# RWKV-7 time mixing: each direction's low-rank product issued by itself, between the preparation's own steps

## The chip, the core and the metric

The kernel runs on one core of one Trainium2 chip. The metric is the device time of one execution in microseconds (us): 2056.7 us is the median of three runs of the kernel before (2055.96 to 2057.23). Five engines of the core are spoken of: PE (TensorE, matmuls), ACT (ScalarE), DVE (VectorE), POOL (GpSimd) and SP (SyncE, which here issues most of the DMA transfers). Each engine works through its own queue in order.

## The reference, cut to what matters

Two trunk layers over 512 latent tokens and 256 context tokens. The first layer's mixer has an RWKV-7 half that runs in both directions `d` (forward, backward). Its preparation computes, per direction, a decay and an in-context learning rate, each through a low-rank product of inner width 64:

```
wl = wl.reshape(bn, s, 2, DECAY_LORA)        # DECAY_LORA = ICLR_LORA = 64
al = al.reshape(bn, s, 2, ICLR_LORA)
w_raw = prm['w0'] + jnp.einsum('bsdl,dlc->bsdc', jnp.tanh(wl), prm['w2'])
decay = jnp.exp(-jnp.exp(-jax.nn.softplus(-w_raw) - 0.5))
iclr = jax.nn.sigmoid(prm['a0'] + jnp.einsum('bsdl,dlc->bsdc', al, prm['a2']))
kk = (k * prm['k_k']).reshape(bn, s, A_HEADS, HEAD_DIM)
kk = kk / jnp.maximum(jnp.sqrt(jnp.sum(kk * kk, axis=-1, keepdims=True)), 1e-12)
```

The scan over the state then uses `w` (decay), `a` (iclr), `kk`, `k`, `r` and `v` of each direction. All the rest (the projections, windowed and other attention, two MLPs, the adaLN vectors from `w_ada`) is not touched.

## The kernel before

**Tiling.** Activations lie feature-major, 128 features on the partitions and T = 768 tokens (512 latent, 256 context) along the free axis. The eight RWKV heads are worked in four passes `p` of two heads (128 features). The two directions' low-rank inputs `wl` and `al` are 128x768 tiles: partitions 0 to 63 hold direction 0, partitions 64 to 127 direction 1. So the product of one direction reads one half of the partitions only.

**The preparation of a pass** is the generator `prep(p)` (L843): it loads `k` and `r` (L849, L850, on SP), forms the heads' inverse norms with `heads_rstd` (ACT square of `k`, L405 matmuls, L854 on DVE, a power on POOL, L412, L415 transposes) and `kk` (L856). Then come the lines of the change, L859 to L886: the low-rank products (L865), tanh and scaling on ACT, two scans on DVE (L877, L879) and the exponentials E and ei on ACT. After the mark FRONT it builds AR and BK (L903 to L908), products L917, the tile N by way of DRAM (L925, L928), and inverts 96 triangular 32x32 matrices in 31 steps of two DVE instructions (L954, L955). After the mark MERGE it joins the inverses (L974, L982 on PE).

**The recurrence of a pass** is `chunks(p)` (L989): four batches of three chunks, each `factors` (L1023 to L1040), `masked` (L1052, L1059), `own` (L1068), `solved` (L1077), and one batch later `local` (L1089, L1099, L1102), `passed` (L1012 to L1015 and, on DVE, L1116) and `step` (L1131 to L1138).

**What runs beside it.** The main loop walks `chunks(p)` and, at fixed rates, takes steps of `prep(p+2)`, of the output of pass p-1, and of `ada` (L332): the adaLN vectors, a product of 80 loads of `w_ada` in this stage, 512 KB each, that the rest of the stage does not need. Each load is one SP transfer (L341) into one of three buffers, is used by one group of four matmuls in the kernel's text (L353; 8 in the trace, where each such matmul stands twice), and every fourth group is followed by L362. I call one such group a filler below. The preparations of passes 0 and 1 run in the stage before, beside the input projection (L430); those of passes 2 and 3 beside `chunks(0)` and `chunks(1)`.

**What sets the order.** The kernel's text only gives a priority. A scheduler places every instruction into its engine's queue ahead of time, by what it expects to be ready; on the chip each queue then runs strictly in that order. In the recurrence stage PSUM has two tiles of two banks (`wide`), one bank for the fillers, and the recurrence's own.

Of the kernel before, what the change touches and what calls it, by code (L numbers as in the profile page):

```python
# [11 lines left out]
F32 = mybir.dt.float32  # L12
F32R = mybir.dt.float32r
AF = mybir.ActivationFunctionType
# [7 lines left out]
L = 512  # L22
CTX = 256
T = L + CTX
# [150 lines left out]
def trunk(ctx: ExitStack, tc: tile.TileContext, xT, cT, vec_d, wada, we, wo_in, wout, wf1, wf2, lw2_d, la2_d, lg2_d,  # L175
          rpb_d, con_d, nm_d, rot_d, out):
    nc = tc.nc
    V, S, G, PE = nc.vector, nc.scalar, nc.gpsimd, nc.tensor
    tt, ts, stt = V.tensor_tensor, V.tensor_scalar, V.scalar_tensor_tensor

    def act(o, i, f=AF.Copy, **k):
        return S.activation(o, i, f, **k)  # L182

    def pool(name, bufs=1, **k):
        return tc.tile_pool(name=name, bufs=bufs, reuse_waits="tile", **k)
# [26 lines left out]
    def one():  # L212
        if PS[0] is None:
            return wide()[:, 0:512]
        return PS[0].tile([128, 512], F32, name="x1")

    def wide():
        return PS[1].tile([128, 1024], F32, name="b2")
# [205 lines left out]
    def product(w, uh, ul, a, b, step=8):  # L424

        hi, lo = w
        ps = one()
        pairs = three(lambda k: hi[:, k, :], lambda k: lo[:, k, :], lambda k: uh[k][:, a:b], lambda k: ul[k][:, a:b], KT)
        for j, (x, y) in enumerate(pairs):
            PE.matmul(ps[:, 0:b - a], x, y, start=j == 0, stop=j == len(pairs) - 1)  # L430
            if j % step == step - 1 and j < len(pairs) - 1:
                yield
        return ps
# [409 lines left out]
    def prep(p, R, rt, iv, sts, res):  # L843

        def tmp():
            return rt.tile([128, T], F32, name="t", bufs=NT0)
# [9 lines left out]
        stt(kk, k, R["kkh"][:, p:p + 1], pb[0][:, :T], op0=ALU.mult, op1=ALU.mult)  # L856
        yield
        E, EI, IC = R["E"], [], []
        def lora(wt, src, bias, outs):  # L859

            ps = [wide() for d in range(2)]
            for a, b in ((0, L), (L, T)):
                for d in range(2):
                    ds = slice(d * 64, d * 64 + 64)
                    PE.matmul(ps[d][:, a:b], wt[ds, p * 128:(p + 1) * 128], src[ds, a:b], start=True, stop=True)  # L865
            for d in range(2):
                act(outs[d], ps[d][:, :T], AF.Tanh, scale=0.5, bias=R["w0h"][:, bias + d * 4 + p:bias + d * 4 + p + 1])
            return outs
        lds = lora(R["lw2"], R["wl"], 0, [tmp() for d in range(2)])
        yield  # L870
        for d in range(2):
            ld = lds[d]
            act(ld, ld, AF.Identity, scale=-0.5 * EM05, bias=R["ldc"])
            yield
            cum = rt.tile([128, T], F32, name=f"ei{d}")
            if d == 0:
                V.tensor_tensor_scan(cum, R["scan"], ld, 0.0, op0=ALU.mult, op1=ALU.add)  # L877
            else:
                V.tensor_tensor_scan(cum[:, ::-1], R["scan"], ld[:, ::-1], 0.0, op0=ALU.mult, op1=ALU.add)  # L879
            yield  # L880
            if not d:
                IC += lora(R["la2"], R["al"], 8, [rt.tile([128, T], F32, name=f"ic{e}") for e in range(2)])
                yield
            act(E[d][:, :, 1:65], c3(cum), AF.Exp)
            act(cum, cum, AF.Exp, scale=-1.0)
            EI.append(cum)  # L886
            yield
# [33 lines left out]
        for d in range(2):  # L921
            for b in range(2):
                o = d * 64 + b * 32
# [26 lines left out]
        for s in range(31):  # L950
            a, b = s + 1, 31 - s
# [10 lines left out]
        for d in range(2):  # L962
            for b in range(2):
                o = d * 64 + b * 32
# [312 lines left out]
    def front(p):  # L1277

        if p < 4:
            preps[p] = prep(p, R, rt, iv, sts, res)  # L1280
            yield from until(preps[p], FRONT)
# [6 lines left out]
    with psum(2, 2), pool("pat", 2, space=PSUM) as pat, pool("wp", side="right") as wp, pool("ub", 1, side="right") as ub:  # L1288
# [127 lines left out]
        R = mix_setup(mixs[1].enter_context(pool("rc")))  # L1416
        btx = ExitStack()
        with pool("po", 1, side="right") as pp:
# [17 lines left out]
            for n, m in enumerate(ms[:3]):  # L1436
                ps = one()
# [9 lines left out]
            while next(cg, "end") != "end":  # L1447
                n += 1
                due += RATE1 if ab else RATE2
                while due >= 1:  # L1450
                    due -= 1
                    if ab and next(ab, "end") == "end":
                        ab = None
                        btx.close()
                        rt, iv = (mixs[q].enter_context(pool(("rt", "iv")[q - 2])) for q in (2, 3))
# [6 lines left out]
            if ab:  # L1462
                drain(ab)
                btx.close()
                rt, iv = (mixs[q].enter_context(pool(("rt", "iv")[q - 2])) for q in (2, 3))
# [281 lines left out]
    with ExitStack() as p3:  # L1747
# [13 lines left out]
        with pool("po", 1) as pp:  # L1761
            ws = [W.take() for _ in range(4)]
            po = [pp.tile([128, T], F32, name=f"po{m}") for m in range(6)]
            for ms, gs in ((range(4), GROUPS[:2]), ((4, 5), GROUPS[:2]), ((0, 1), GROUPS[2:])):
                for c, tok in gs:
                    while c == 1 and pend:
                        tick()
                    for m in ms:
                        if m == len(ws):
                            ws.append(W.take())  # L1770
                        p = product(ws[m], *u1, tok.start, tok.stop, 12)
# [119 lines left out]
```

## Time and profile before

| what | value |
|---|---|
| three runs, median (lowest, highest) | 2056.7 us (2055.96, 2057.23) |
| the profiled execution, its own time | 2055.19 us |
| span of that execution | 2053.4 us |
| mean granted clock of TensorE | 0.971 |
| PE busy | 1932.7 us, 94% of the span |
| DVE / ACT / POOL busy | 1124.7 / 817.0 / 122.2 us |
| recurrence of pass 0 / 1 / 2 / 3 begins (first L974) | 357.0 / 448.3 / 549.9 / 622.3 us |
| the output stage's first matmul (L1588) | 691.3 us |

The profile page gives busy times over the whole span; since stages differ, the rows quoted further down are taken by stretches of time, given in us from the start of the span. "[0.96 <-DVE t L412]" behind a row means that the engine sat idle for 0.96 us just before it, and that the wait ended with that instruction. A matmul row with xN merges N instructions. Names in the rows are the program's tile names without their buffer numbers. The L numbers are lines of the kernel before.

### The profile page before, as it was taken

How to read it: one execution, taken by the hardware profiler on the slowest of the kernel's cores; microseconds unless marked ns; L12 is line 12 of the kernel's file. 1: busy time of each engine (PE TensorE's matmuls, PEld its weight loads, DVE VectorE, ACT ScalarE, POOL GpSimd, SP SyncE). 2: the span in 40 equal slices, each digit the busy share in tenths (PEclk: the TensorE clock that was granted, in tenths of full speed). 3: DMA queues.
4: the chain of work that ended last, by engine and by line, in shares of the span. 5: the costliest groups of instructions: out<-in, count | busy, mean ns of one | idle time of the engine just before them, and what ended most of it. 6: DMA issues, size and time to landing. Idle time of an engine off the chain costs nothing.

```text
span 2053.4 us, 38620 instructions
## 1 busy us (share of the span) xinstructions
PE 1932.7 (94%) x16412; PEld 1633.5 (80%) x16412; DVE 1124.7 (55%) x1999; ACT 817.0 (40%) x1531; POOL 122.2 (6%) x149
## 2 busy tenths in 40 slices
PE   6999988988888899999999999899999899999997
PEld 3878767666666897888888889898888798888887
DVE  6576477547464377233433345856575575444445
ACT  3466442534335244311322122435686645222332
POOL 1000011011100000000000000001021000000000
PEclk9999989999999999999999999999999999999998
DMA  7422334666634233211221021342111334322221
GB/s 309 149 65 78 108 109 129 209 195 207 207 126 145 71 112 132 73 61 42 83 72 62 32 83 42 103 151 68 51 39 37 123 102 166 102 83 82 97 88 42
DMA packets 112013, 217.47 MB, mean 106 GB/s; under 512 B 38496, under 2 KB 63968, under 8 KB 111328
## 3 DMA queue, kind: packets, MB, share of 16 engines
q1 hardware_dynamic: 96544, 191.66, 28.6%
q10 hardware_dynamic: 15296, 23.33, 3.2%
q8 instruction: 129, 2.11, 0.4%
q14 instruction: 44, 0.36, 0.1%
HBM read 184.29 MB, written 28.05 MB: 103 GB/s over the span
## 4 chain that ended last, share of the span: by engine, by line
PE 63%; DVE 7%; ACT 3%; issue 3%; DMA 2%; POOL 1%; POOLq 0%; ACTq 0%; DVEq 0%; SPq 0%
PE x L1588 45%; PE x L430 5%; PE ax L530 2%; PE ax L511 2%; PE b L1015 1%; PE b L493 1%; PE ad L353 1%; PE b L1077 1%; PE b L494 1%; DMA w_raw<-in_wada_dram 1%; DVE X L955 1%; DVE nacc L288 1%; ACT Z L182 1%; DVE pr L954 1%; POOL r L264 0%
## 5 line engine op out<-in xcount | busy, mean ns | idle before, releaser
L182 ACT ACTIVATE w_hi<-w_raw 128x1024 fp32r<-128x1024 f32 x183 | 192.3, 1058 | 484.1 <-PE x L1588 369.1
L225 DVE TENSOR_TENSOR w_lo<-w_raw,w_hi 128x1024 fp32r<-128x1024 f32 x181 | 220.8, 1223 | 194.6 <-ACT w_hi L182 193.0
L1588 PE MATMUL x<-fl,w_hi 128*128 128x256 f32 (+1 forms) x864 | 290.9, 338 | 3.9 <-DVE fl L1675 3.9
L1588 PE MATMUL x<-uh,w_hi 128*128 128x512 f32 (+1 forms) x864 | 286.7, 337 | 3.0 <-ACT uh L182 3.0
L1588 PE MATMUL x<-fh,w_lo 128*128 128x256 f32 (+1 forms) x864 | 289.4, 336 | 0.0
L1588 PE MATMUL x<-ul,w_hi 128*128 128x512 f32 (+1 forms) x864 | 287.9, 336 | 0.0
L1588 PE MATMUL x<-uh,w_lo 128*128 128x512 f32 (+1 forms) x864 | 287.6, 336 | 0.0
L1588 PE MATMUL x<-fh,w_hi 128*128 128x256 f32 (+1 forms) x864 | 286.9, 337 | 0.0
L1602 DVE TENSOR_TENSOR oa<-x,oa 128x512 f32<-128x512 f32 (+1 forms) x184 | 103.1, 563 | 207.9 <-PE x L1588 207.0
L430 PE MATMUL x<-uh,w_hi 128*128 128x256 f32 (+1 forms) x560 | 190.2, 340 | 1.6 <-ACT po L182 1.3
L430 PE MATMUL x<-uh,w_lo 128*128 128x256 f32 (+1 forms) x560 | 189.1, 338 | 0.0
L430 PE MATMUL x<-ul,w_hi 128*128 128x256 f32 (+1 forms) x560 | 188.5, 337 | 0.0
L1588 PEld LDWEIGHTS x<-fl,w_hi 128*128 128x128 f32 x864 | 164.3, 190 | 22.0 <-DVE fl L1675 4.3
L1588 PEld LDWEIGHTS x<-uh,w_hi 128*128 128x128 f32 x864 | 161.8, 189 | 21.1 <-ACT uh L182 3.9
L1588 PEld LDWEIGHTS x<-fh,w_lo 128*128 128x128 f32 x864 | 164.1, 190 | 17.9
L1588 PEld LDWEIGHTS x<-fh,w_hi 128*128 128x128 f32 x864 | 162.1, 190 | 20.0 <-ACT fh L182 2.5
L1588 PEld LDWEIGHTS x<-ul,w_hi 128*128 128x128 f32 x864 | 162.8, 189 | 17.7
L1588 PEld LDWEIGHTS x<-uh,w_lo 128*128 128x128 f32 x864 | 162.8, 189 | 17.6
L430 PEld LDWEIGHTS x<-uh,w_hi 128*128 128x128 f32 x560 | 107.5, 192 | 12.5 <-issue 2.7
L430 PEld LDWEIGHTS x<-uh,w_lo 128*128 128x128 f32 x560 | 107.7, 192 | 9.4 <-issue 1.2
L430 PEld LDWEIGHTS x<-ul,w_hi 128*128 128x128 f32 x560 | 107.8, 192 | 9.2 <-issue 1.3
L1674 DVE TENSOR_TENSOR rl<-rl 128x512 f32<-128x512 f32 (+1 forms) x108 | 59.3, 550 | 77.7 <-ACT fh L182 77.5
(304 smaller groups left out, 3398.7 us busy)
## 6 DMA issues: line engine op xcount, KB each, us to landing
w_raw<-in_wf_dram SPq DMA_DIRECT2D x128, 512.0 KB
w_raw<-in_wada_dram SPq DMA_DIRECT2D x96, 512.0 KB
w_raw<-in_we_dram SPq DMA_DIRECT2D x21, 512.0 KB
w_raw<-in_wo_in_dram SPq DMA_DIRECT2D x18, 512.0 KB
w_raw<-in_wout_dram SPq DMA_DIRECT2D x16, 512.0 KB
hsc<-h ACTq DMA_DIRECT2D x8, 1024.0 KB
scr<-po ACTq DMA_DIRECT2D x21, 384.0 KB
h<-hsc SPq DMA_DIRECT2D x7, 1024.0 KB
```

The costliest lines, as they stand in the source:

```text
L182: return S.activation(o, i, f, **k)
L225: eng.tensor_tensor(o_lo, x, o_hi.bitcast(F32), op=ALU.subtract)
L288: V.tensor_reduce(acc, sq.rearrange("p k t -> p t k"), axis=AX.X, op=ALU.add)
L353: PE.matmul(ps[o:o + 32, 0:256], si[:, 2 * kp + k, :], w[:, k, j * 256:(j + 1) * 256], start=kp == 0, stop=kp == 3)
L430: PE.matmul(ps[:, 0:b - a], x, y, start=j == 0, stop=j == len(pairs) - 1)
L493: PE.matmul(ps[:, off:off + n], qs, kh, start=True, stop=False)
L494: PE.matmul(ps[:, off:off + n], qs, kl, start=False, stop=True)
L511: PE.transpose(pt[:, (kb - k0) * 128:(kb - k0 + 1) * 128], P[:, kb * 128:(kb + 1) * 128], ident)
L530: PE.matmul(po[h * 64:h * 64 + 64, 0:128], v(h, k), pts[h][:, k], start=k == 0, stop=k == n - 1)
L1588: PE.matmul(o, a, b, start=n == 0, stop=n == len(pairs) - 1)
L1602: tt(oa[:, m, tok], ps, oa[:, m, tok], op=ALU.add)
L1674: tt(r, r, r, op=ALU.mult)
```

## The change

`lora` computed one kind of product for both directions: four matmuls, the two directions in turn for the 512 and then the 256 columns, into two `wide` tiles, followed by both tanh. It now computes one direction: two matmuls into one `wide` tile and one tanh. The decay product of direction 1 is issued after the whole chain of direction 0 instead of before it, and each direction's learning-rate product follows its own scan. The number of matmuls, activations, scans and steps (`yield`) is the same.

```
-        def lora(wt, src, bias, outs):
-            ps = [wide() for d in range(2)]
-            for a, b in ((0, L), (L, T)):
-                for d in range(2):
-                    ds = slice(d * 64, d * 64 + 64)
-                    PE.matmul(ps[d][:, a:b], wt[ds, p * 128:(p + 1) * 128], src[ds, a:b], start=True, stop=True)
-            for d in range(2):
-                act(outs[d], ps[d][:, :T], AF.Tanh, scale=0.5, bias=R["w0h"][:, bias + d * 4 + p:bias + d * 4 + p + 1])
-            return outs
-        lds = lora(R["lw2"], R["wl"], 0, [tmp() for d in range(2)])
-        yield
         for d in range(2):
-            ld = lds[d]
+            ds = slice(d * 64, d * 64 + 64)
+            def lora(wt, src, bias, o):
+                ps = wide()
+                for a, b in ((0, L), (L, T)):
+                    PE.matmul(ps[:, a:b], wt[ds, p * 128:(p + 1) * 128], src[ds, a:b], start=True, stop=True)
+                act(o, ps[:, :T], AF.Tanh, scale=0.5, bias=bias)
+                return o
+            ld = lora(R["lw2"], R["wl"], R["w0h"][:, d * 4 + p:d * 4 + p + 1], tmp())
             act(ld, ld, AF.Identity, scale=-0.5 * EM05, bias=R["ldc"])
             yield
...
-            if not d:
-                IC += lora(R["la2"], R["al"], 8, [rt.tile([128, T], F32, name=f"ic{e}") for e in range(2)])
-                yield
+            IC.append(lora(R["la2"], R["al"], R["w0h"][:, 8 + d * 4 + p:8 + d * 4 + p + 1], rt.tile([128, T], F32, name=f"ic{d}")))
+            yield
             act(E[d][:, :, 1:65], c3(cum), AF.Exp)
```

The scheduler places the rest of the stage anew. Lines behind the change carry numbers that are lower by five now (L1077 is L1072, L1099 is L1094, L1102 is L1097).

**Place 1, SP, from the load of `v` of pass 0 on.** `k`, `r` and `v` are loads of the recurrence and of the preparation of pass 2, `lg` and `gl` of the gate, `nscr` and `N` the way of pass 1's tile through DRAM, `w_raw<-in_wada` the loads of the fillers. Before:

```order
L1000 DMA v<-scr 128x768
L849 DMA k<-scr 128x768
L836 DMA lg_3421<-in_lg_dram 128x512
L838 DMA gl<-scr 128x768
L341 DMA w_raw<-in_wada_dram 128x1024 x2
L925 DMA nscr<-XI 32x24x32 x4
L341 DMA w_raw<-in_wada_dram 128x1024 x2
L928 DMA N<-nscr 96x1024
L341 DMA w_raw<-in_wada_dram 128x1024 x7
L850 DMA r<-scr 128x768
```

The same place on SP now:

```order
L995 DMA v<-scr 128x768
L836 DMA lg_3421<-in_lg_dram 128x512
L838 DMA gl<-scr 128x768
L341 DMA w_raw<-in_wada_dram 128x1024
L920 DMA nscr<-XI 32x24x32 x4
L341 DMA w_raw<-in_wada_dram 128x1024 x2
L923 DMA N<-nscr 96x1024
L341 DMA w_raw<-in_wada_dram 128x1024 x8
L849 DMA k<-scr 128x768
L850 DMA r<-scr 128x768
```

The load of `k` of pass 2, second in this row before, now stands behind eleven more filler loads; counted from the program's start, seven filler loads stand ahead of it before, and eighteen now.

**Place 2, PE, in `chunks(0)`, from the end of the first batch (`solved`) on.** L405 is the product of `heads_rstd` of pass 2, which reads the square of that `k`. Before:

```order
L1077 MATMUL b_3868<-XA,XI 64x128 x12
L405 MATMUL b_3886<-con,t 128x2 x6
L1023 MATMUL b_3903<-con,bk_2657 128x128 x3
L1023 MATMUL b_3903<-con,bk_2658 128x128 x3
L1099 MATMUL py<-Z,BT 64x64
L1029 MATMUL b_3913<-con,ar 128x128 x3
L1040 MATMUL b_3913<-con,vr 128x128 x3
L1099 MATMUL py<-Z,BT 64x64
L415 MATMUL b_3930<-con,t 128x128
```

The same place on PE now:

```order
L1072 MATMUL b_3868<-XA,XI 64x128 x12
L1094 MATMUL py<-Z,BT 64x64 x2
L353 MATMUL ad<-w_raw,si 32x256 x4
L1094 MATMUL py<-Z,BT 64x64 x2
L1097 MATMUL py<-Z,BT 64x64 x8
L353 MATMUL ad<-w_raw,si 32x256 x12
L362 MATMUL ad<-con,adar 128x4 x2
L353 MATMUL ad<-w_raw,si 32x256 x16
L362 MATMUL ad<-con,adar 128x4 x2
L353 MATMUL ad<-w_raw,si 32x256 x8
L405 MATMUL b_3886<-con,t 128x2 x6
L1018 MATMUL b_3903<-con,bk_2657 128x128 x3
```

Ten fillers (40 matmuls of the text) in one row now stand between `solved` and L405, where none stood; fillers 9 to 18 of the stage. Nine fillers precede L405 before, eighteen now. At the next such place, L405 of pass 3, the count is 46 in both.

**Place 3, PE, in the second batch of `chunks(0)`: the low-rank products of pass 2.** Two `wide` tiles at once before (b_4091 is direction 0, b_4092 direction 1):

```order
L1068 MATMUL b_4069<-Z,AK 64x64 x5
L865 MATMUL b_4091<-al,la_469 128x512
L865 MATMUL b_4092<-al,la_469 128x512
L865 MATMUL b_4091<-al,la_469 128x256
L353 MATMUL ad<-w_raw,si 32x256 x4
L865 MATMUL b_4092<-al,la_469 128x256
```

The same place on PE now (b_4061 is `al` of direction 0, b_4106 `wl` of direction 1):

```order
L1010 MATMUL b_4039<-BT,XA 64x128 x8
L865 MATMUL b_4061<-al,la_469 128x512
L865 MATMUL b_4061<-al,la_469 128x256
L1063 MATMUL b_4069<-Z,AK 64x64 x12
L362 MATMUL ad<-con,adar 128x4 x2
L1126 MATMUL pd<-Nb,MQ 64x64
L865 MATMUL b_4106<-wl,lw_468 128x512
L353 MATMUL ad<-w_raw,si 32x256 x4
L865 MATMUL b_4106<-wl,lw_468 128x256
L1072 MATMUL b_4111<-XA,XI 64x128 x12
```

In passes 2 and 3 all four products now stand apart, with other work between them. In passes 0 and 1 the scheduler puts `al` of direction 0 and `wl` of direction 1 next to each other, so two of the four products still have a neighbour on the other half of the partitions.

## Rows read from the trace of the kernel before

**Rows 1.** The page: the PE line of its first part, the GB/s line of its second (40 equal slices of the span), and the shares by engine of the chain that ended last.

```profile
PE 1932.7 (94%) x16412; PEld 1633.5 (80%) x16412; DVE 1124.7 (55%) x1999; ACT 817.0 (40%) x1531; POOL 122.2 (6%) x149
...
GB/s 309 149 65 78 108 109 129 209 195 207 207 126 145 71 112 132 73 61 42 83 72 62 32 83 42 103 151 68 51 39 37 123 102 166 102 83 82 97 88 42
...
PE 63%; DVE 7%; ACT 3%; issue 3%; DMA 2%; POOL 1%; POOLq 0%; ACTq 0%; DVEq 0%; SPq 0%
```

**Rows 2.** Busy time by stretches of the recurrence stage: the stretch, its length, busy us (instructions) of PE, PEld, DVE, ACT, POOL, then the granted clock, the DMA share and GB/s.

```profile
357.00:374.00 17.00, 14.71 (x349) 12.09 (x345) 4.80 (x10) 8.09 (x16) 0.46 (x2) 0.70 0.66 182
...
392.00:420.00 28.00, 25.80 (x446) 17.52 (x444) 22.81 (x61) 13.14 (x24) 0.37 (x1) 1.00 0.82 275
...
374.00:478.00 104.00, 91.60 (x1704) 62.91 (x1702) 60.31 (x141) 43.30 (x83) 12.86 (x13) 0.97 0.69 213
...
625.00:691.00 66.00, 56.08 (x1218) 45.93 (x1218) 31.92 (x42) 34.84 (x60) 4.87 (x5) 0.92 0.32 108
```

**Rows 3.** The low-rank products alone (L865) by stretches: PE busy us (instructions), PEld, granted clock, DMA share, GB/s. First one product of one direction of pass 0 by itself, then all four of pass 1, then the two pairs of pass 2 and the two pairs of pass 3.

```profile
253.00:255.50 2.50, 1.55 (x4) 0.67 (x4) 0.99 0.00 0
287.00:300.00 13.00, 9.83 (x16) 4.47 (x16) 0.51 0.03 12
382.00:386.00 4.00, 1.89 (x8) 0.66 (x8) 1.00 0.65 198
396.00:400.00 4.00, 2.47 (x8) 1.07 (x8) 1.00 0.76 253
491.00:494.00 3.00, 2.21 (x8) 1.15 (x8) 1.00 0.54 175
500.00:504.00 4.00, 2.68 (x8) 0.97 (x8) 1.00 0.67 241
```

**Rows 4.** PE in order of time: start, us, instruction, count, and in brackets the idle time before it and what ended it. Two low-rank products of pass 0; the end of the first batch of `chunks(0)` and the start of the second; a wait later in `chunks(0)`; and the same places of `chunks(1)`.

```profile
249.38 1.22 PE L865 MATMUL b<-wl,lw 64*128 64x512 f32 x1
...
249.39 1.22 PE L865 MATMUL b<-al,la 64*128 64x512 f32 x1
...
372.53 1.53 PE L1077 MATMUL b<-XA,XI 64*64 64x128 f32 x24 [0.59 <-ACT XA L182]
373.99 1.17 PE L405 MATMUL b<-con,t 128*128 128x2 f32 x9
...
376.55 0.33 PE L1099 MATMUL py<-Z,BT 128*64 128x64 f32 x2
...
378.91 0.30 PE L415 MATMUL b<-con,t 128*128 128x128 f32 x1 [0.96 <-DVE t L412]
...
382.21 0.63 PE L1102 MATMUL py<-Z,BT 128*64 128x64 f32 x15
...
432.17 0.38 PE L1131 MATMUL pd<-x,MQ 64*64 64x64 f32 x5 [2.23 <-DVE MQ L1116]
...
467.52 1.53 PE L1077 MATMUL b<-XA,XI 64*64 64x128 f32 x24
...
470.07 0.33 PE L1099 MATMUL py<-Z,BT 128*64 128x64 f32 x2 [0.21 <-ACT Z L182]
...
478.23 2.67 PE L405 MATMUL b<-con,t 128*128 128x2 f32 x12 [1.26 <-ACT t L182]
```

**Rows 5.** SP in order of time (start, us over which the merged issues lie, what is issued): `k` of pass 2, filler loads, and the store of pass 1's inverses.

```profile
350.23 0.34 SPq L849 DMA_DIRECT2D k<-scr  x1
...
354.27 2.06 SPq L341 DMA_DIRECT2D w_raw<-in_wada_dram  x2
...
364.14 25.55 SPq L341 DMA_DIRECT2D w_raw<-in_wada_dram  x7
...
414.49 0.34 SPq L959 DMA_DIRECT2D xscr<-X  x1
```

**Rows 6.** The chain that ended last, in order of time: start, us, what; transfers that work waited for from issue to landing.

```profile
441.54 5.57 DMA w_raw<-in_wada_dram
...
473.30 3.92 DMA k<-scr
...
542.33 4.47 DMA w_raw<-in_wada_dram
...
583.99 5.76 DMA w_raw<-in_wada_dram
```

**Rows 7.** What PE waited for from 374 to 478 us: us in total, times, longest.

```profile
PE ad L353 <- DMA w_raw<-in_wada_dram: 3.4, 4, 1.3
PE pd L1131 <- DVE MQ L1116: 2.6, 2, 2.2
```

**Rows 8.** The last reader of pass 1's `k` on POOL, the square of pass 2's `k` on ACT, and the first step of pass 1's inverse on DVE, in order of time.

```profile
348.40 1.80 POOL L940 TENSOR_TENSOR t<-ic,k 128x768 f32<-128x768 f32 x1 [8.69 <-DVE bk L908]
...
353.38 0.94 ACT L182 ACTIVATE t<-k,vec 128x768 f32<-128x768 f32 x1 [3.91 <-DVE ar L945]
...
381.44 0.18 DVE L954 TENSOR_TENSOR pr<-X,N 96x31 f32<-96x31 f32 x1
```

**Rows 9.** The fillers alone from 374 to 478 us: the matmuls L353, and in the second row L362; the columns of Rows 3.

```profile
374.00:478.00 104.00, 24.32 (x296) 6.02 (x296) 0.97 0.69 213
...
374.00:478.00 104.00, 5.37 (x36) 4.70 (x36) 0.97 0.69 213
```

## The prediction

> **What bounds the kernel now.** I read the page first, then stretches, then PE in order of time. PE is busy 94% of the span and holds 63% of the chain that ended last [rows 1]; the shares don't tell what a change inside one stage is worth, so the stretches come next. From 374 to 478 us, where the preparation of pass 2 runs beside `chunks(0)`, PE is busy 91.6 of 104 us; in the last pass, with no filler left, 56.1 of 66 [rows 2]. The stage therefore ends with PE's work plus PE's gaps, and those gaps are short: 3.4 us on filler loads and 2.6 on the tile MQ in these 104 us [rows 7]. The other engines have room, DVE 60 of 104 us [rows 2]. Whatever lengthens PE's work here, or stops its queue, delays every later stage one for one, since PE goes on to the output stage in the same queue.
>
> **Part 1: the products lose their neighbour.** One direction's product alone takes 1.55 us at the full clock (2.4 GHz), so four apart take 6.2. Side by side, the two pairs of pass 2 take 1.89 + 2.47 = 4.36 us and those of pass 3 2.21 + 2.68 = 4.89 [rows 3]. Apart, the passes gain 1.84 and 1.31 us of PE work, 3.15 in all. Passes 0 and 1 gain nothing: in pass 0 `wl` of direction 1 and `al` of direction 0, two separate calls, already ran at the same time (249.38 and 249.39) [rows 4], and they stay neighbours; in pass 1 all four take 9.83 us at half clock [rows 3], two pairs' worth of overlap before and one before the other in the new order alike. The bounds of this part are 0 (it falls into gaps) and 3.15; I take 3.15, since PE has few gaps at these places.
>
> The rows say that a pair costs 1.89 to 2.68 us where one product costs 1.55, so the overlap is partial. The Trainium skill ("TensorE: Matmul & The Clock Gate", Measured speedup vs the span model) would let row-packed matmuls finish in the time of one plus some 4 ns for each further tile. By that page a pair would take 1.55 us and the split would cost 3.1 us a pass, an estimate of 6.2 in all instead of 3.15; no pair here shows it, and the measurement decides.
>
> What the split may win: one `wide` tile at a time instead of both, an earlier tanh, shorter holds of the `t` buffers. The trace has no gap of note that these would end, so 0. In pass 0 DVE gets two L945 ahead of L903 and L908 of direction 1, up to 1 us of wait for L917; with direction 0's BK earlier in exchange I take 0, between -1 and +1.
>
> **Part 2: the load of `k` moves, and PE's queue stops for it.** Before, `k` of pass 2 was issued at 350.23, right after its buffer's last reader on POOL, and its square was ready at 354.3 [rows 5, 8], 20 us before PE came to L405 at 373.99 [rows 4]. Now SP issues it behind eleven more filler loads. A filler load waits until a buffer is given back by the filler three places earlier, so SP cannot reach `k` until PE has done filler 15. On PE fillers 9 to 18 stand in a row ahead of L405, and behind L405 everything waits: L1023 and all of the second batch on PE; on ACT the square of `k` stands ahead of that batch's BT; on DVE the norm stands amid pass 1's inverse.
>
> Walk it through. Only three filler buffers exist, so fillers 9, 10 and 11 have their data and 12 to 18 must be loaded within the row. PE reaches the end of `solved` some 1.0 us earlier, since one filler at half clock moved behind it: L1077 starts at 371.5. L1099 starts 2.55 us after the start of L1077, as in `chunks(1)` (467.52, 470.07) [rows 4]: 374.05; filler 9 is done and its buffer free by 375.0. A load takes 4.47 to 5.76 us from issue to landing where work waited for it [rows 6]; take 4.5: 379.5. The next six follow at the pace of the DMA: 0.524 MB at 275 GB/s, the rate of the busiest stretch [rows 2], is 1.9 us each: 390.9. `k` (0.393 MB) takes 1.4 us more: 392.3; its square 0.94 [rows 8]: L405 starts at 393.2, 19.2 us later than before. By then PE has done ahead of time nine fillers at 24.32 / 37 = 0.66 us, two groups L362 at 5.37 / 9 = 0.60 [rows 9], and L1099 and L1102, some 1.2 us [rows 4]: 8.3 us. The stall is 19.2 - 8.3 = 10.9 us net.
>
> Bounds: with 3.92 us to the first landing [rows 6], 309 GB/s [rows 1], so 1.7 us each, and `k` landing with the last load, L405 starts at 390.0 and 7.7 us are lost. With 5.76, 2.1 us each (three buffers, (5.76 + 0.66) / 3) and 3.92 for `k` after the last load, it starts at 398 and 15.9 are lost. I take 10.9, nearest to the busiest measured stretch.
>
> Here the rate is what a page would price otherwise. The rows show 275 GB/s in the busiest stretch. The Trainium skill ("DMA: Bandwidth & Descriptors", Anatomy of one DMA) fits a transfer as 2.0 us plus its bytes at 436 GB/s. By that, an estimate, a load lands 3.2 us after its issue and the next ones 1.2 apart, L405 starts at 387.2 and the stall is 4.9 us; the loads of 4.5 to 5.8 us in this trace speak against it.
>
> **What is given back, and the clock.** The same number of fillers lies between here and L405 of pass 3, so 9 fewer come later. Of PE's 12.4 us of gaps in these 104 us some end: a filler now stands by the 2.23 us wait for MQ [rows 4], two of the waits around L362 move into the row, and pass 1's inverse, which started at 381.44 behind `kk` of pass 2 [rows 8] and was stored at 414.49 [rows 5], is done before the second batch and leaves DVE free. But `chunks(1)` starts with fewer fillers to cover its own waits. Between 0 and 9 us; I take 4. The clock: after a wait of 1.26 us and others before it L405 of pass 3 took 2.67 us [rows 4], and the stretch from 357 to 374 had a granted clock of 0.70, a mix of 2.4 and 1.2 GHz [rows 2]. Behind 10 us of idling the first work will run at 1.2 GHz: 0 to 5 us, I take 1.2, the excess of that one L405.
>
> **The sum.** 3.15 + 10.9 + 1.2 - 4 = 11.3 us. The profiled execution took 2055.2 us, so 2066.5; the median of the runs stands 1.5 above it: 2068. The ends: 0 + 7.7 + 0 - 9 gives no loss, which I count with the rivals; 3.15 + 7.7 + 0 - 9 = 1.9, so 2058.6; 3.15 + 15.9 + 5 - 0 = 24, so 2081.
>
> **The rivals.** (a) The burst runs faster than its neighbours in the trace: nothing else is under way on the DMA, loads follow at 1.7 us, `k` lands with the last. 7.7 + 3.15 - 3.2 = +7.6: 2064. For it: the transfers of 309 GB/s at the start; against it: 4.5 us and more to landing wherever work waited. The page's fit above points this way. (b) The stall is moved, not added: the gaps behind it close, since fillers are then far ahead and DVE is free. 10.9 + 3.15 - 9 = +5, and with the faster burst +2: 2059 to 2062. Against it: most gaps are waits within the recurrence that no filler covers. (c) The other side: the early inverse and the burst buy back more than they cost. It decides where the gaps ended exceed the stall plus the products' excess: with a stall of 7.7, the products hidden, and all 12.4 us of gaps gone, 4.7 us faster: 2052. Against it: `chunks(1)` followed `chunks(0)` without waiting for the inverse, so an earlier one brings nothing by itself. (d) Worse: `k` lands late behind `r` and the loads, and the clock stays at 1.2 GHz for ten microseconds more: +18 to +24: 2075 to 2081. (e) The queue's new order does nothing, since loads run far enough ahead: 2057. Three buffers speak against it.
>
> **How the numbers follow.** A measurement of this kernel can tell some 0.2%, 4.1 us, from no change. Forecast 0.48, (a) 0.15, (b) 0.16, (c) 0.07, (d) 0.10, (e) 0.04. Slower by over 0.2%: 0.48 + 0.15 + 0.10 and half of (b), 0.81; within: half of (b) and (e), 0.12; faster: 0.07. The range takes in the forecast's bounds, (a), (b) and most of (d): 2058 to 2079.
>
> **What would show it.** Right: L405 of pass 2 near 393 us, behind fillers that wait for `w_raw`, the row from L1077 to L405 with some 10 us of idle PE; products of 1.55 us each in passes 2 and 3; `chunks(1)` and all later stages 10 to 12 us later. Wrong: L405 before 385, or the start of the output stage near 691 in spite of a late L405 (gaps closed), or fillers that start without a wait.

## The result, and the profile after

| | kernel before | changed kernel |
|---|---|---|
| median of 6 runs each (lowest, highest) | 2055.93 us (2052.72, 2057.23) | 2075.64 us (2068.53, 2080.87) |
| ratio, 95% interval | | 1.0103, 1.0086 to 1.0119 |
| profiled execution, its own time; span; clock | 2055.19; 2053.4; 0.971 | 2068.53; 2066.4; 0.964 |
| `chunks(0)` begins (first L974, now L969) | 357.1 us | 360.1 us |
| L405 of pass 2 | 374.0 | 394.3 |
| `chunks(1)` begins | 448.3 | 464.1 |
| `chunks(2)` begins | 549.9 | 564.1 |
| `chunks(3)` begins | 622.3 | 635.1 |
| output stage begins (L1588, now L1583) | 691.35 | 706.49 |

Slower, by 19.7 us in the medians, within the range. The execution that left the profile was the shortest of its six: 13.3 us longer than the profiled one of before. The table says where these 13.3 us arise: 3.0 are there when the recurrence begins, 12.7 come in `chunks(0)`, the rest stays within 2.5 us a stage in both signs. Not all of the 12.7 is lost time: six fillers and one L362, some 4.6 us at the rates of [rows 9], are done in `chunks(0)` now and later before (five of the six in `chunks(1)`, one in `chunks(2)`).

The place that the prediction walked through, PE in order of time, answering to [rows 4]:

```profile
373.02 1.53 PE L1072 MATMUL b<-XA,XI 64*64 64x128 f32 x24 [0.59 <-ACT XA L182]
375.56 0.33 PE L1094 MATMUL py<-Z,BT 128*64 128x64 f32 x2 [1.02 <-ACT Z L182]
...
377.63 1.07 PE L353 MATMUL ad<-w_raw,si 128*32 128x256 f32 x16
380.19 0.64 PE L353 MATMUL ad<-w_raw,si 128*32 128x256 f32 x8 [1.49 <-DMA w_raw<-in_wada_dram]
381.34 0.61 PE L362 MATMUL ad<-con,adar 128*128 128x4 f32 x4 [0.50 <-ACT adar L182]
382.91 2.30 PE L353 MATMUL ad<-w_raw,si 128*32 128x256 f32 x16 [0.97 <-DVE X L950]
385.59 1.08 PE L353 MATMUL ad<-w_raw,si 128*32 128x256 f32 x8 [0.38 <-DMA w_raw<-in_wada_dram]
388.08 1.08 PE L353 MATMUL ad<-w_raw,si 128*32 128x256 f32 x8 [1.41 <-DMA w_raw<-in_wada_dram]
...
391.07 2.31 PE L353 MATMUL ad<-w_raw,si 128*32 128x256 f32 x16 [0.33 <-DVE mod L364]
394.29 2.72 PE L405 MATMUL b<-con,t 128*128 128x2 f32 x12 [0.91 <-ACT t L182]
396.87 1.52 PE L1018 MATMUL b<-con,bk 128*128 128x128 f32 x6
```

Eleven filler loads now stand ahead of `k` on SP, as the order said. SP in order of time, answering to [rows 5], where `k` was issued at 350.23:

```profile
366.26 20.80 SPq L341 DMA_DIRECT2D w_raw<-in_wada_dram  x8
387.11 0.42 SPq L849 DMA_DIRECT2D k<-scr  x1
387.59 1.48 SPq L850 DMA_DIRECT2D r<-scr  x1
```

The first load of the row let its filler start at 380.19 (forecast 379.5), `k` landed 6.10 us after its issue at 387.11 (chain of waits: "387.11 6.10 DMA k<-scr"), at 393.2 (forecast 392.3), and L405 started at 394.29 (forecast 393.2). But the fillers end at 391.07 + 2.31 = 393.38 too: row and load end together. L405 stands behind the row in PE's queue and starts behind it in the trace, so the row alone keeps it back until 393.38; the square of `k`, for which PE then waits 0.91 us, would have kept it back until 394.29 without the row as well. What PE waited for in the row, from the end of L1072 at 374.55 to 394.29 us (us in total, times, longest):

```profile
PE ad L353 <- DMA w_raw<-in_wada_dram: 3.3, 3, 1.5
PE py L1094 <- ACT Z L182: 1.2, 2, 1.0
PE ad L362 <- ACT adar L182: 1.1, 2, 0.6
PE ad L353 <- DVE X L950: 1.0, 1, 1.0
PE b L405 <- ACT t L182: 0.9, 1, 0.9
PE ad L353 <- DVE mod L364: 0.3, 1, 0.3
```

That is 7.8 us of waits in 19.74, not ten, since most fillers take 1.08 us here where one takes 0.64 at the full clock. (L353 reads no X, so the load is the likelier end of the wait put down to X L950.)

The clock, from windows of 2 us of the changed kernel (stretch, length, then busy us of PE, PEld, DVE, ACT, POOL, granted clock, DMA share, GB/s):

```profile
380.00:382.00 2.00, 1.25 (x12) 0.68 (x12) 0.00 (x0) 0.38 (x1) 0.00 (x0) 1.00 0.86 303
...
384.00:386.00 2.00, 1.49 (x12) 0.41 (x16) 1.83 (x6) 0.00 (x0) 0.00 (x0) 0.50 0.79 221
...
398.00:400.00 2.00, 1.67 (x8) 1.27 (x6) 0.31 (x1) 1.11 (x2) 1.82 (x2) 0.60 0.00 0
400.00:402.00 2.00, 1.61 (x22) 1.06 (x24) 1.90 (x6) 1.42 (x4) 0.45 (x1) 1.00 0.00 0
```

PE falls to 1.2 GHz between 382 and 384, after fillers with waits between them, and is back at 2.4 GHz only between 398 and 400, behind L405 and L1018 to L1035, which all ran at 1.2.

The 3.0 us ahead of the recurrence come from a place where the prediction took nothing, the preparation of pass 0. PE in order of time there, in the changed kernel:

```profile
249.56 2.93 PE L865 MATMUL b<-al,la 64*128 64x512 f32 x4
252.41 0.79 PE L430 MATMUL x<-uh,w_hi 128*128 128x512 f32 x1
253.01 0.63 PE L430 MATMUL x<-ul,w_hi 128*128 128x512 f32 x1
253.56 2.93 PE L865 MATMUL b<-wl,lw 64*128 64x512 f32 x4
...
257.14 2.93 PE L865 MATMUL b<-al,la 64*128 64x512 f32 x4
...
262.73 0.56 PE L430 MATMUL x<-uh,w_hi 128*128 128x512 f32 x1
263.12 0.40 PE L430 MATMUL x<-ul,w_hi 128*128 128x512 f32 x1
```

`al` of direction 0 and `wl` of direction 1, which started within 0.01 us of each other in [rows 4], now have two L430 between them. Before, the last matmul of the two products was this one:

```profile
251.69 0.63 PE L865 MATMUL b<-al,la 64*128 64x256 f32 x1
```

It ended at 252.32, so both together took 2.94 us from 249.38 on, where one by itself takes 2.93 at this clock. L430 takes 0.63 us at 1.2 GHz and 0.40 at 2.4, so the clock returns at 262.7 now. In the kernel before it returned at 253 (windows of the kernel before, same columns):

```profile
250.00:252.00 2.00, 2.00 (x8) 0.69 (x4) 1.63 (x1) 0.00 (x0) 0.00 (x0) 0.50 0.36 141
252.00:254.00 2.00, 2.00 (x6) 1.08 (x5) 0.00 (x0) 1.66 (x3) 0.00 (x0) 0.74 0.00 0
254.00:256.00 2.00, 2.00 (x8) 1.24 (x7) 1.93 (x4) 2.00 (x4) 0.00 (x0) 1.00 0.00 0
```

The lone products of passes 2 and 3, windows of L865 alone (busy us of PE, PEld, granted clock, DMA share, GB/s), answering to [rows 3]:

```profile
400.00:412.00 12.00, 3.11 (x8) 1.34 (x8) 1.00 0.42 137
412.00:420.00 8.00, 3.29 (x8) 1.18 (x8) 1.00 0.76 221
420.00:424.00 4.00, 0.35 (x2) 0.00 (x0) 1.00 1.02 174
...
503.00:510.00 7.00, 1.63 (x4) 0.74 (x4) 0.83 0.42 144
510.00:514.00 4.00, 1.55 (x4) 0.67 (x4) 1.00 0.41 141
514.00:520.00 6.00, 1.55 (x4) 0.67 (x4) 1.00 0.61 193
520.00:530.00 10.00, 1.55 (x4) 0.67 (x4) 1.00 0.65 205
```

6.75 us in pass 2 and 6.28 in pass 3, against 4.36 and 4.89: +3.8 us of PE work where the prediction had +3.15. The four products of pass 0 take 11.70 us where they took 7.42, and those of pass 1 take 9.83 in both kernels.

### The profile page after: what moved, and what is told of

Read it like the earlier page. It is cut to its first block, busy times and chain, and to the rows that moved or that the text cites. A ratio compares the mean times of both kernels' runs of the same rounds, so it can differ in the third digit from the quotient of the medians.

```text
span 2066.4 us, 38617 instructions
## 1 busy us (share of the span) xinstructions
PE 1947.0 (94%) x16412; PEld 1641.4 (79%) x16412; DVE 1125.6 (54%) x1999; ACT 818.0 (40%) x1531; POOL 121.0 (6%) x149
## 4 chain that ended last, share of the span: by engine, by line
PE 79%; DVE 8%; issue 5%; ACT 4%; DMA 2%; POOL 1%; SPq 0%; ACTq 0%; POOLq 0%; DVEq 0%
PE x L1583 45%; PE x L430 11%; PE ax L530 3%; PE ax L511 2%; PE b L493 2%; PE ad L353 2%; PE b L865 1%; PE b L494 1%; PE b L1010 1%; PE b L1072 1%; DMA w_raw<-in_wada_dram 1%; POOL r L264 1%; ACT Z L182 1%; PE ax L531 1%; DVE nacc L288 1%
## 5 line engine op out<-in xcount | busy, mean ns | idle before, releaser
L1583 PE MATMUL x<-fl,w_hi 128*128 128x256 f32 (+1 forms) x864 | 291.7, 339 | 3.9 <-DVE fl L1670 3.9
L1583 PE MATMUL x<-fh,w_lo 128*128 128x256 f32 (+1 forms) x864 | 290.1, 337 | 0.0
L1583 PE MATMUL x<-uh,w_hi 128*128 128x512 f32 (+1 forms) x864 | 286.8, 337 | 3.0 <-ACT uh L182 3.0
L1583 PE MATMUL x<-ul,w_hi 128*128 128x512 f32 (+1 forms) x864 | 287.7, 336 | 0.0
L1583 PE MATMUL x<-uh,w_lo 128*128 128x512 f32 (+1 forms) x864 | 287.4, 335 | 0.0
L1583 PE MATMUL x<-fh,w_hi 128*128 128x256 f32 (+1 forms) x864 | 287.3, 338 | 0.0
L1597 DVE TENSOR_TENSOR oa<-x,oa 128x512 f32<-128x512 f32 (+1 forms) x184 | 103.1, 563 | 207.5 <-PE x L1583 206.9
L430 PE MATMUL x<-uh,w_hi 128*128 128x256 f32 (+1 forms) x560 | 190.8, 341 | 1.3 <-ACT po L182 1.0
L430 PE MATMUL x<-uh,w_lo 128*128 128x256 f32 (+1 forms) x560 | 189.8, 339 | 0.0
L430 PE MATMUL x<-ul,w_hi 128*128 128x256 f32 (+1 forms) x560 | 188.9, 337 | 0.0
L1583 PEld LDWEIGHTS x<-fl,w_hi 128*128 128x128 f32 x864 | 165.2, 191 | 22.0 <-DVE fl L1670 4.5
L1583 PEld LDWEIGHTS x<-fh,w_lo 128*128 128x128 f32 x864 | 164.9, 191 | 17.8
L1583 PEld LDWEIGHTS x<-uh,w_hi 128*128 128x128 f32 x864 | 161.6, 189 | 21.2 <-ACT uh L182 3.9
L1583 PEld LDWEIGHTS x<-fh,w_hi 128*128 128x128 f32 x864 | 162.6, 191 | 19.9 <-ACT fh L182 2.5
L1583 PEld LDWEIGHTS x<-ul,w_hi 128*128 128x128 f32 x864 | 162.7, 189 | 17.8
L1583 PEld LDWEIGHTS x<-uh,w_lo 128*128 128x128 f32 x864 | 162.6, 189 | 17.6
L430 PEld LDWEIGHTS x<-uh,w_hi 128*128 128x128 f32 x560 | 107.8, 192 | 12.3 <-issue 2.6
L430 PEld LDWEIGHTS x<-uh,w_lo 128*128 128x128 f32 x560 | 107.8, 193 | 10.2 <-issue 1.8
L430 PEld LDWEIGHTS x<-ul,w_hi 128*128 128x128 f32 x560 | 108.0, 193 | 9.3 <-issue 1.3
```

The costliest lines, as they stand in the source:

```text
L1583: PE.matmul(o, a, b, start=n == 0, stop=n == len(pairs) - 1)
L1597: tt(oa[:, m, tok], ps, oa[:, m, tok], op=ALU.add)
```

## The experiments

The theory, from here on "the row": the ten fillers that the new order puts ahead of L405 of pass 2 stop PE for loads, and the low clock lengthens what stands there and behind. Beside it: the low clock in pass 0. The rivals: the load of `k` itself holds L405; or the lone products cost what is lost. Each kernel ran in five rounds beside the kernel before, whose median was 2054.7 us beside e1 to e4, 2052.3 beside e5 to e8 and 2054.7 beside e9 to e12; so the ratio, with its 95% interval, is what counts. In the diffs the lines marked "..." stand for the changed form and, behind `else`, for that of before.

**e1: the change in passes 0 and 1 only.**

```diff
+        if p in (0, 1):
...
+        else:
...
```

> The changed form (one direction's product by itself) in passes 0 and 1 only; passes 2 and 3 have the pairs of before. In the order SP issues k of pass 2 behind eighteen filler loads and PE has the ten fillers ahead of L405, both as in the changed kernel. Theory 'row of fillers': all of the stall stays and only the products' excess of passes 2 and 3 (3.15 us) goes: 2064 to 2072, L405 of pass 2 at 392 to 396 us. Rival 'products': what costs is the lone products of passes 2 and 3, so within 4 us of before, 2056 to 2060.

Measured: 2070.49 us, ratio 1.0079 (1.0058 to 1.0101); in its trace L405 of pass 2 at 392.9. With the pairs of before in passes 2 and 3, most of the loss is there. The lone products there are not the cause.

**e2: the change in passes 2 and 3 only** (`if p in (2, 3):`, as in e1).

> The changed form in passes 2 and 3 only. In the order k of pass 2 and L405 stay where they were before (seven filler loads ahead of k, nine fillers ahead of L405). Theory 'row of fillers': only the products' excess, +3.15 us: 2058 to 2061, L405 of pass 2 at 374 us, chunks(0) longer by 1.8 us. Rival 'products': 2065 or more.

Measured: 2050.10 us, ratio 0.9978 (0.9965 to 0.9991); L405 of pass 2 at 372.7. Neither theory said this: with lone products in passes 2 and 3 the kernel is 4.5 us faster. e9 repeats it.

**e3: the change in pass 0 only** (`if p in (0,):`).

> The changed form in pass 0 only; the order is that of before from pass 1 on. Theory 'clock in pass 0': the lone product of direction 1 of wl no longer stands beside al of direction 0, TensorE stays at 1.2 GHz from 244 to 263 us instead of to 253, and the recurrence begins 3 us late: 2058 to 2060. Rival 'no cost in pass 0' (as the prediction had it): 2055 to 2057.

Measured: 2058.59 us, ratio 1.0027 (1.0013 to 1.0040): 5.5 us by the ratio. In its trace the clock is at 0.50 from 250 to 262 and 0.62 from 262 to 264. The cost in pass 0 is real. What it is made of, e3 does not part: `wl` of direction 1 runs by itself, and the clock comes back later.

**e4: `k` from POOL's queue.**

```diff
-        nc.sync.dma_start(k, scr[3 + 3 * p + 1])
+        nc.gpsimd.dma_start(k, scr[3 + 3 * p + 1])
```

> The changed kernel with the load of k issued from POOL's queue, so that no filler load stands ahead of it; the ten fillers still stand ahead of L405 on PE. If the load of k holds L405 (as the prediction had it), L405 comes near 382 to 386 us at the latest and the time is 2056 to 2062. If the row of fillers on PE holds it, the data of k being there by 365 us changes almost nothing: L405 at 392 to 394 us, 2066 to 2075.

Measured: 2071.22 us, ratio 1.0072 (1.0050 to 1.0093), L405 at 399.5, later than either reading had it. The load of `k` goes out early, POOL in order of time:

```profile
350.95 1.80 POOL L935 TENSOR_TENSOR t<-ic,k 128x768 f32<-128x768 f32 x1 [7.82 <-DVE bk L903]
353.05 0.62 POOL L849 DMA_DIRECT2D k<-scr  x1 [0.30 <-POOL t L935]
```

and yet PE stands in the row, which the scheduler has put one step earlier, ahead of L1035, whose operand `vr` is made from `v`. SP now issues `v` at 385.18, behind the same fillers, eight of whose loads take from 370.74 to 385.13 to be issued. PE in order of time:

```profile
376.62 1.08 PE L353 MATMUL ad<-w_raw,si 128*32 128x256 f32 x8 [2.60 <-DMA w_raw<-in_wada_dram]
378.96 1.08 PE L353 MATMUL ad<-w_raw,si 128*32 128x256 f32 x8 [1.26 <-DMA w_raw<-in_wada_dram]
...
386.29 0.64 PE L353 MATMUL ad<-w_raw,si 128*32 128x256 f32 x8 [1.55 <-DMA w_raw<-in_wada_dram]
...
390.68 1.08 PE L353 MATMUL ad<-w_raw,si 128*32 128x256 f32 x8 [0.72 <-DMA w_raw<-in_wada_dram]
392.19 0.90 PE L1035 MATMUL b<-con,vr 128*128 128x128 f32 x3 [0.42 <-POOL vr L1033]
...
399.46 1.50 PE L405 MATMUL b<-con,t 128*128 128x2 f32 x12
```

So `k` is not needed for the stall: with its data there long before, PE still waits for the loads of the fillers, and what is queued behind the row comes late. The kernel is not a clean test in one point: `v` took the place of `k`, so a row with nothing queued behind it was not seen.

**e5: the changed kernel again**, for a second trace and for the spread of its runs.

> The changed kernel once more, beside the others of this call, for a second trace and for its spread: 2066 to 2081, with L405 of pass 2 at 392 to 396 us again. If the spread of its runs (2068.5 to 2080.9) is the clock, a longer run shows a lower granted clock in the recurrence and the same waits; if it is the filler loads, it shows longer waits of L353.

Measured: 2070.54 us (2064.84 to 2081.32), ratio 1.0097 (1.0070 to 1.0124), L405 at 397.6, in a run in which L405 of pass 0 was already 2.5 us later. The profiled run took 2072.68 us. From L405 of pass 2 to `chunks(1)` it needed 75.0 us, the first trace 69.8, though PE is idle for 4.5 us there and for 4.4 in the first. Windows of this kernel:

```profile
384.00:386.00 2.00, 1.29 (x12) 0.75 (x12) 0.97 (x4) 0.19 (x1) 0.00 (x0) 0.84 0.96 363
386.00:388.00 2.00, 1.48 (x12) 0.20 (x8) 1.83 (x6) 0.00 (x0) 0.00 (x0) 0.50 0.77 274
...
404.00:416.00 12.00, 12.00 (x138) 7.90 (x140) 8.68 (x20) 4.57 (x8) 0.00 (x0) 0.50 0.34 122
416.00:418.00 2.00, 2.00 (x22) 1.01 (x16) 1.90 (x6) 0.46 (x1) 0.00 (x0) 0.98 0.15 49
```

The clock comes back at 416, 18 us behind the start of L405, in the first trace some 5 us behind it. That is what parts the two traces here: same order, as much waiting, but another time at 1.2 GHz. Of the twelve runs of the changed kernel the four shortest (up to 2068.9 us) have a mean clock of 0.964 to 0.966, the two longest 0.958 and 0.959. But the kernel before, without the row, spreads as widely (2046.5 to 2061.0 us beside e5), so the spread by itself says nothing about the row.

**e6: the changed kernel with two buffers for `k`.**

```diff
-        k = rt.tile([128, T], F32, name="k")
+        k = rt.tile([128, T], F32, name="k", bufs=2)
```

> The changed kernel with two buffers for k in place of one, which is all that differs; k no longer waits for POOL's last reader of the k before it, and the order has six filler loads ahead of k of pass 2, eight fillers ahead of L405 and none between solved and L405, as before the change. Theory 'row of fillers': the 12 to 13 us of chunks(0) go; what remains is the clock in pass 0 (about +4) and what e2_split23 showed (about -4): 2052 to 2060, L405 of pass 2 at 376 to 380 us. Rival 'the lone products or the order of the steps are slow in themselves': 2066 or more.

Measured: 2053.38 us, ratio 1.0006 (0.9988 to 1.0023). SP issues `k` of pass 2 at 319.60; PE goes from `solved` to L405 as it did before the change:

```profile
370.94 1.53 PE L1072 MATMUL b<-XA,XI 64*64 64x128 f32 x24 [0.59 <-ACT XA L182]
372.40 1.50 PE L405 MATMUL b<-con,t 128*128 128x2 f32 x12
```

The loss is gone with the row, while the change's steps and products all remain. How much of it a second buffer gains by itself is the question of e12. The preparation of pass 0 still takes its 3 us more (table below).

**e7: the change in passes 1, 2 and 3** (`if p in (1, 2, 3):`).

> The changed form in passes 1, 2 and 3; pass 0 as before, where wl of direction 1 and al of direction 0 stand next to each other. The order keeps k and L405 where they were before. If pass 0's lone products and the row of fillers are all that costs, this is as fast as e2_split23, 2048 to 2054, L405 of pass 1 at 282 to 284 us. If a split in pass 1 costs as the one in pass 0 does, 2053 to 2058.

Measured: 2053.64 us, ratio 1.0007 (0.9993 to 1.0021), L405 of pass 1 at 284.9. No different from before, and so 6 us slower than e2 and e9, which differ from it in pass 1 alone. Where the split of pass 1 itself stands, it costs nothing: from L405 of pass 1 to `chunks(0)` the traces of e7, e2 and e9 all take 74.1 us, that of before 74.4. What stands out in e7's trace is the stretch from L405 of pass 2 to `chunks(1)`, 79.6 us and the longest of all (table below); why is open.

**e8: the change in pass 2 only** (`if p in (2,):`).

> The changed form in pass 2 only. The term of the prediction for lone products says +1.84 us: 2056 to 2058. If e2_split23's gain of 4.5 us is real and lies in pass 2, 2049 to 2053; if it lies in pass 3, 2054 to 2058.

Measured: 2054.85 us, ratio 1.0016 (1.0001 to 1.0032): 3.3 us slower, barely clear of noise. Here the term for lone products (1.84 forecast) has its sign.

**e9: e2 again, and e10: the change in pass 3 only** (`if p in (3,):`).

> The kernel of e2_split23 once more (changed form in passes 2 and 3 only). If its gain of 0.2% is real, the ratio lies at 0.9965 to 0.999 again; if lone products there are worth nothing either way, 0.999 to 1.001; if the prediction's term of 3.15 us is right, 1.0015.

> The changed form in pass 3 only. The prediction's term says +1.3 us, 1.0006; with e8_split2 at 1.0016, a real gain in e2_split23 would have to lie here, at 0.996 to 0.998.

Measured: e9 2051.67 us, 0.9976 (0.9963 to 0.9989); e10 2050.70 us, 0.9980 (0.9965 to 0.9995). The gain of e2 repeats and comes with pass 3, some 4 us (e7, with pass 1 split as well, doesn't show it). It lies where the traces can't settle it: `chunks(2)`, behind the products of pass 3, is 66.7 us long in e10, 67.3 in e9, 70.4 in e2 and 72.4 before. Some 1.3 us of this is moved and not saved: in e2, e9 and e10 two fillers that stood in `chunks(2)` are done in `chunks(1)`. First the kernel before, then e10, `chunks(2)`:

```profile
549.93:622.34 72.41, 63.70 (x1316) 47.61 (x1311) 40.32 (x102) 25.17 (x53) 7.35 (x8) 0.95 0.52 153
```

```profile
548.20:614.80 66.60, 59.25 (x1297) 45.32 (x1294) 39.63 (x100) 25.04 (x53) 8.33 (x8) 1.00 0.56 155
```

In e10 it ran at the full clock throughout, in e9 at 0.95 as before, so the clock is part of it at most.

**e11: e9 with two buffers for `k`; e12: the kernel before with two buffers for `k`**, the edit of e6.

> The changed form in passes 2 and 3 and two buffers for k. Fillers ahead of L405 of pass 2 as before the change, four fewer ahead of L405 of pass 3, whose k is now loaded some forty loads earlier. If the wait of 1.26 us for the square of k and the low clock behind it at L405 of pass 3 are worth something, 1 to 4 us faster than e9_split23_again; else the same.

> The kernel before with two buffers for k and nothing else changed. Control for e6_two_k_buffers: if the second buffer by itself gains as much as the changed kernel lost, some 15 us, then e6 shows nothing about the row of fillers. The theory says it gains 0 to 3 us here (the wait at L405 of pass 3): 0.9985 to 1.000.

Measured: e11 2050.26 us, 0.9986 (0.9973 to 0.9999); e12 2043.92 us, 0.9952 (0.9937 to 0.9967). e11 gained nothing on e9. In its trace `chunks(1)` is 10.6 us shorter than in e9's, and `chunks(2)` and `chunks(3)` are 6.5 and 4.8 longer: it is given back. Part of this is moved work: six fillers and one L362, some 4.6 us, which e9 does in `chunks(1)` and e11 in `chunks(2)`. e12 beats both kernels, and more than was expected. Before, `k` of pass 3 was issued at 473.30 and L405 waited for its square and took 2.67 us [rows 4]; now it is issued at 352.97, and PE in order of time reads:

```profile
471.08 0.49 PE L1040 MATMUL b<-con,vr 128*128 128x128 f32 x3
471.54 1.50 PE L405 MATMUL b<-con,t 128*128 128x2 f32 x12
```

As a control for e6 it is less clean than hoped: a second buffer gains 10.7 us by the medians, 9.9 by the ratio, even where there was no row. Where it gains them is not settled. `chunks(1)`, whose L405 has four fillers fewer ahead of it and no wait, is 6.1 us shorter than before. But `chunks(0)` is 5.0 shorter too, and 3.8 of these lie ahead of L405 of pass 2, where the clock was 1.00 in this trace and 0.70 before; e10, whose order there is that of before, also had 1.00 and was 3.1 shorter. In e6 the order leaves `k` and L405 of pass 3 where they were (46 filler loads of the stage ahead of that `k` in the changed kernel and in e6, 7 in e12). So e6 shows that the loss goes with the row, but not that all of its 17 us is the row's. The kernels with one buffer show the row without this question: those that have it stand at 1.0072 to 1.0103 (changed kernel, e1, e4, e5), those that don't at 1.0027 or less (e2, e3, e7 to e10).

All the traces together, in us. Pass 0 is the time from its L405 to the start of `chunks(0)`:

| kernel | pass 0 | `chunks(0)` to L405 of pass 2 | from there to `chunks(1)` | `chunks(1)` | `chunks(2)` | `chunks(3)` |
|---|---|---|---|---|---|---|
| before | 118.3 | 16.9 | 74.3 | 101.6 | 72.4 | 69.0 |
| changed | 121.1 | 34.2 | 69.8 | 100.0 | 71.0 | 71.4 |
| e5, the same again | 121.4 | 34.7 | 75.0 | 100.3 | 70.4 | 68.6 |
| e1, passes 0, 1 | 121.6 | 33.8 | 73.4 | 98.3 | 71.6 | 68.6 |
| e4, `k` from POOL | 116.0 | 42.0 | 69.0 | 93.4 | 71.5 | 73.2 |
| e3, pass 0 | 123.1 | 15.6 | 75.5 | 103.1 | 70.9 | 68.6 |
| e6, two `k` buffers | 121.8 | 14.4 | 77.5 | 101.4 | 68.1 | 69.8 |
| e7, passes 1, 2, 3 | 117.9 | 16.4 | 79.6 | 101.2 | 66.0 | 68.7 |
| e8, pass 2 | 118.4 | 16.4 | 77.5 | 99.1 | 69.7 | 69.3 |
| e2, passes 2, 3 | 118.0 | 16.2 | 74.1 | 103.1 | 70.4 | 69.0 |
| e9, the same again | 118.0 | 15.8 | 75.0 | 102.3 | 67.3 | 68.9 |
| e10, pass 3 | 117.7 | 13.8 | 75.3 | 101.2 | 66.7 | 70.2 |
| e11, e9 with two | 118.0 | 16.8 | 75.3 | 91.7 | 73.8 | 73.7 |
| e12, before with two | 118.4 | 13.2 | 73.1 | 95.5 | 69.7 | 71.2 |

Two columns part the kernels without overlap. The first: 117.7 to 118.4 where pass 0 has the form of before, 121.1 to 123.1 where it has the new one, with e4 as the exception (its order differs in the preparations as well). The second: 13.2 to 16.9 without the row, 33.8 to 42.0 with it. Without the row its spread goes with the granted clock of that stretch: 1.00 in e10 and e12, 0.88 in e6, 0.78 in e3 and e9, 0.68 to 0.70 in the other five. In the columns behind it kernels with the same order there differ by up to 5 us (changed and e5), so a difference of that size between two traces means little.

## Why the prediction was right, and where it was not

**The stall.** Right in place, cause and size. Loads that follow at the pace of the DMA were taken at 1.9 us; fillers 12 and 16 start behind waits for their loads at 380.19 and 388.08, four loads in 7.9 us, 1.97 each. L405 is 17.3 us later in its stage (34.2 against 16.9), forecast 19.2; less the 8.3 us of work done ahead of time, at the prediction's own prices, the net stall is 9.0, forecast 10.9. That L405 waits for `k` was only half of it: the row of fillers alone keeps PE until 393.38, and e4 has the row's waits with `k` long there. The Trainium skill ("DMA: Bandwidth & Descriptors", Anatomy of one DMA) fits transfers issued by GpSimd, while SP issues these; by that fit, an estimate, loads would follow every 1.2 us and L405 start at 387, which does not agree with these rows.

**What is given back.** 4 us were taken, between 0 and 9, and that is what PE's gaps gave: from L405 to `chunks(1)` PE was idle for 8.5 us before, and for 4.4 and 4.5 in the two traces of the changed kernel (its waits for MQ, 2.6 us in [rows 7], are 0.5). The time shows less of it. The changed kernel is 4.5 us shorter there in one trace and 0.7 longer in the other, though it has three fillers and one L362 fewer to do; PE's clock was 0.96 and 0.88 there, 1.00 before. The other six of the nine fillers done ahead are missed in `chunks(1)`, ahead of L405 of pass 3.

**The clock** was the term that is too small: 1.2 us, bounds 0 to 5, for one L405. PE stayed at 1.2 GHz for some 17 us in the one trace (382 to 384, to 398 to 400) and some 31 in the other (385 to 416), and 5 and 18 us of that lie behind the row, on work that the sum had at full clock but for L405. The measured median lies 7.6 us above the forecast, in the band of rival (d), 2075 to 2081, which had a chance of 0.10, and the clock behind the row is (d)'s mechanism. That it is the reason why the medians lie 18 to 20 us above those of before where the sum said 11.3 is not shown. The longer of the two traces and the mean clocks speak for it, but no run had the row without the low clock, the cost in pass 0, below, takes its share, and e4, whose clock was 1.00 from L405 to `chunks(1)`, lost 0.7% all the same. The Trainium skill ("TensorE: Matmul & The Clock Gate", HAM oscillation) describes kernels whose groups of matmuls are shorter than the waits for DMA between them and start each group at the low clock. Ahead of the fall the trace agrees: from 378.70 to 382.91 PE waited for 2.96 us, 1.49 of them for one load, and worked for 1.25. Behind it the clock stayed low though the fillers, 1.08 us each, are mostly longer than the waits of 0.3 to 1.4 between them. How long the work behind such a row stays at the low clock is what the two traces differ on, by 13 us.

**Pass 0** is the step that failed. "They stay neighbours" was read off the list of low-rank products; the order itself has two L430 between them, and the prediction's own row (249.38 and 249.39) showed what that neighbour was worth. The products of pass 0 take 4.3 us more: 2.9 because the two no longer run at the same time, 1.4 because the last one runs at 1.2 GHz instead of 2.4, as does all the work up to 262.7. From L405 of pass 0 to L405 of pass 1 it is 43.9 us in all traces with the form of before and 47.9 to 48.3 with the new one (e4: 45.0). At the start of `chunks(0)` 2.9 of this is left in the trace, and e3 lost 5.5 by the ratio. For pass 1 the prediction held: 9.83 us before and after.

**The products' 3.15 us.** The PE work is there (+3.8), the time is not: +3.3 us for pass 2 alone (e8), -4 for pass 3 alone (e10), -5 for both (e2, e9). "PE has few gaps at these places" does not hold for pass 3. In the changed kernel none of this gain is seen: e1 is at 1.0079, the changed kernel at 1.0097 to 1.0103. The parts don't add: e1 and e9 would make 1.0055. "No pair here shows it", said of two products that finish in the time of one, overlooks the pair of pass 0: 2.94 us for both, 2.93 for one. The pairs of passes 2 and 3, from which the 3.15 was taken, had other work between their matmuls or did not start together.

**Luck.** That the sum came within 8 us owes something to terms that cancel: pass 0, put at 0, cost 2.9 to 5.5 us, and the products of passes 2 and 3, put at 3.15, cost nothing together (e2, e9). In rival (a) the -3.2 stands where the sum's own terms, 1.2 - 4, make -2.8; nothing hangs on it.

**Left open.** That the scheduler puts the row there because it expects POOL's last reading of `k` late is argued from e6, where a second buffer takes the row away; what it expects is in no trace. Neither the form in pass 0 alone (e3) nor that in passes 1 to 3 (e7) moves the load of `k`; in passes 0 and 1 together it does (e1). Why pass 3 gains is open, as is why e7 doesn't, and why e11 gives its gain back and e12 does not, beyond the fillers that move.

## What to carry to other kernels

An edit that changes no work can still move a queue: compare the order on each engine, and ask of every run of fill-in work whether its own loads can keep up, because an in-order engine stops for work that nobody needs yet. When a load is needed early but its single buffer is given back late, a second buffer may be the cheapest edit there is; here it removed the loss of the change, and on the kernel before it gained 0.5%. And look at the clock behind a stall as well as at its wait: here the work behind it ran at 1.2 GHz for another 5 to 18 us.

## What the runs showed of the hardware

- Behind a row of short matmuls with waits between them TensorE came back to 2.4 GHz some 5 us after the start of L405 in one run and 18 us after it in another, with the same instructions in the same order. In the second PE had no gap from 404 to 416 us and stayed at 1.2 GHz throughout.
- A lone product of one direction (64 of 128 partitions) takes 2.93 us at 1.2 GHz and 1.55 at 2.4; two that start within 0.01 us of each other on the two halves of the partitions took 2.94 together at 1.2. In pass 0 the clock returned at 253 behind the pair and one L430, and without the pair at 262.7, behind six L430 in a row.
- 29 runs of the kernel before, beside e5 to e8, spread over 14 us (2046.5 to 2061.0), the shortest with a mean clock of 0.976, the longest with 0.968.
